# A hybrid encoder block on one core: three split weights in store, and a fourth Strassen pair in each FFN's second output part

## The chip, the cores and the metric

The kernel runs on one core of one Trainium2 chip. The metric is the device time of one execution in microseconds (us); the time of a kernel is the median of its runs.

## The reference, cut to what matters

One layer of an encoder with 256 tokens of width 2048, all in float32:

```python
h = layer_norm(ALPHA * h + 0.5 * swiglu_ffn(h, ffn1_w_in[l], ffn1_w_out[l]), ...)
mix = hybrid_mixer(h, w_in[l], ...)          # attention A, attention B, gates
h = layer_norm(ALPHA * h + mix, ...)
xa = memory_cross_attention(h, mem, ...)
h = layer_norm(ALPHA * h + xa, ...)
h = layer_norm(ALPHA * h + 0.5 * swiglu_ffn(h, ffn2_w_in[l], ffn2_w_out[l]), ...)

def swiglu_ffn(x, w_in, w_out):              # w_in 2048 x 11008, w_out 5504 x 2048
    g, u = jnp.split(x @ w_in, 2, axis=-1)
    return (jax.nn.silu(g) * u) @ w_out
```

## The kernel before, in words

Every weight is read once. A weight step is a tile `raw` of 128 x 2048 float32 (1 MB), loaded on SyncE's queue (L191, three buffers). ScalarE rounds it to `hi` in fp32r, two casts of 1024 columns (L262), and VectorE forms `lo = raw - hi` (L265). TensorE then computes hi x hi, hi x lo and lo x hi. The hi and lo of one step are a unit; `UNITS` (L51) is how many are held. Method `run` (L177) takes the list of steps in order and decides before each step which later weights are split already: at most `UNITS` units live, and at most two weights ahead of the next one. With two units that is one weight ahead of the one in use. A list scheduler then sets each engine's order from this program and the priorities.

An ordinary step (`mm_pair`, L301, matmuls at L309) handles two k-tiles for two column groups and both token halves: 24 matmuls of 512 columns. At some steps a Strassen form in Winograd's variant (`mm_sums`, L345, matmuls at L363) takes 21. For it VectorE forms sums of the weight's four blocks (`weight_sums`, L246 and L248), splits the weight's last 1536 columns and the 2048 of sums (`X` in the blocks X2 and X3), and forms sums of the activations (`sum_forms`, L319, L323, and L254 for their lo). Four of the seven products go to banks of their own; after the last Strassen step of a group they are copied and added (`shared`, L674 to L679), and then added to the residual (L628). The other matmuls gather in four banks, added to it at the end (`finish`, L749).

Each FFN (`ffn`, L551) has two halves of 24 and 19 k-tiles of its hidden width. A half is made of input groups (8 steps each, Strassen at 2, 4 and 6), whose products become hidden activations (`hidden`, L720 to L723), and of output parts. The second half's output is in two parts: the first 1024 columns by `out_pair` (L616) in ten steps of two k-tiles, the last of one, Strassen at 3, 5 and 7 (`SUMS_OUT`, L30); the other 1024 by `out_proj` (L755, matmuls at L296). The first part is what this document calls the output part; its activations' forms lie in the blocks X1 (steps 3 and 5) and X0 (step 7). `pair_group` (L643) walks the steps of a group in the order of the k-tiles.

Small tiles `w1` (128 x 256, L137) hold the totals of queries and keys, the rotary key's steps and some activations' forms. GpSimd issues the loads of biases, gains, rotary tables and memory tokens.

Of the kernel before, what the change touches and what calls it, by code (L numbers as in the profile page):

```python
# [27 lines left out]
SUMS_IN = {2: ("X0", 0), 4: ("X0", 1), 6: None}  # L28
AT_FIRST = 4, 6
SUMS_OUT = ({3: ("X1", 0), 5: ("X1", 1), 7: ("X0", 0), 9: ("X0", 1)},  # L30
            {3: ("X1", 0), 5: ("X1", 1), 7: ("X0", 0)})
SUMS_YB = {4: ("T0", 0), 6: ("T0", 1), 2: None}
AT_YB = (2, 4, 6), (4, 6)
SUMS_XQ = {4: ("H5", 0), 6: ("H5", 1), 2: None}
# [5 lines left out]
SUM_HOME = ("X2", "X3"),  # L40
# [7 lines left out]
RMS_EPS = 1e-6  # L48
NEG = -1e30
MAGIC = 0x5F3759DF  # L50
UNITS = 2  # L51
SOON, NEAR, LATE = 400, 100, -400
WARM = 9
HEADS = ("H4", "H5", "X2", "X3")
# [45 lines left out]
class Kernel:  # L100
    def __init__(self, ctx, tc, t, out):
        self.tc, self.nc, self.t, self.out = tc, tc.nc, t, out

        def pool(name, bufs=1, **kw):
            return ctx.enter_context(tc.tile_pool(name=name, bufs=bufs, **kw))

        self.const = pool("const")
        self.wraw = pool("wraw", 3)
        self.whi = pool("whi", UNITS)
        self.wlo = pool("wlo", UNITS)  # L110
        self.blocks = pool("blocks")
# [22 lines left out]
        return self.work.tile(list(shape), dt, tag="w2", bufs=6, name=self.name("w2"))  # L134

    def w1(self, shape=(P, S), dt=F32):
        return self.work.tile(list(shape), dt, tag="w1", bufs=6, name=self.name("w1"))  # L137

    def sm(self, tag, n, dt=F32, bufs=None):
        return self.small.tile([P, n], dt, tag=tag, name=self.name(tag), **({"bufs": bufs} if bufs else {}))  # L140
# [36 lines left out]
    def run(self):  # L177
# [3 lines left out]
        def slots(w):  # L181
            return 0 if isinstance(w, tuple) and w[1] else 1
# [35 lines left out]
        def early(w):  # L218
            return not isinstance(w, Sums) and w[1] is not None and "early" in w[1]

        def ahead(need, held):
            if nxt < need:
                return True
            n = sum(not early(w) for w in queue[need:nxt])
            return (nxt < need + 5 and (early(queue[nxt]) or n < 2)
                    and held + live + slots(queue[nxt]) <= UNITS)

# [323 lines left out]
    def ffn(self, tag, xT, st, first=None, steps=None, late=None, before=None, tags=None):  # L551


        t = self.t
        f0 = bank = 0
        turn = None
        fx = {}
        for half, nf in enumerate(F_SPLIT):
            hid, fh, homes = Act([]), {}, SUMS_OUT[half]
            end = half == len(F_SPLIT) - 1  # L560
            form = lambda c, fh=fh, homes=homes, hid=hid: self.forms_step(fh, homes, c, lambda: hid)
            for g in range(-(-nf // 4)):
                j, n = f0 // 4 + g, min(4, nf - 4 * g)
                qs, ps = {}, {}
                if j == 2 and first is not None:
                    self.add(self.load_rest)
                if j == 0 and first is not None:
                    main, (ps, qs, fx) = [], first
                    self.add(lambda qs=qs: self.shared(qs, 512), prio=SOON)
                elif j == 0 and before:  # L570
                    main = self.collect(self.first_group, tag, xT, before, ps, fx)
                else:
                    src = t[tag + "_w_in"][j] if n == 4 else t[tag + "_w_in_r"][0]
                    main = self.collect(self.pair_group, bank, src, n * P, KT, xT, SUMS_IN, fx, ps, qs, None, SUM_HOME + ("H5",))
                if turn and n < 4:
                    turn[5] = turn.pop(6)
                self.weave(main, turn or {}, prio=0)
                for c, (home, _) in homes.items():
                    if home == "X1" and c // 2 == g - 1:
                        self.add(form(c))  # L580
                hidden, turn = self.hidden(ps, bank, g, n, hid, qs)
                self.add(hidden, prio=SOON)
                if before and 2 <= j < 6:
                    self.add(lambda q=j - 2: self.gb_apply(2, self.h, (q,)), prio=LATE)
                if j == 0 and first is not None:
                    for c in set(SUMS_IN) - set(AT_FIRST):
                        self.add(self.forms_step(fx, SUMS_IN, c, xT, False))
                bank ^= 1
            if end and late:
                self.add(lambda: setattr(self, "cut", True))  # L590

            def out(hid=hid):
                x = lambda: hid
                src = [t[tag + "_w_out"][g, :, f0 * 1024:(f0 + nf) * 1024] for g in range(2)]
                self.out_pair(bank, src[0], 0, nf, x, homes, fh, half == 0, st if end else None,
                              SUM_HOME + ("H5",) if end else SUM_HOME)
                if end:
                    self.out_proj(tag + "_w_out_r", nf, x, False, st, steps, tags, 2, cut=tags is None)
                else:
                    self.out_pair(bank ^ 1, src[1], 1, nf, x, homes, fh, half == 0, None)  # L600
            main = self.collect(out)

            side = dict(turn)
            if end and late:
                side[len(main) - 6] = [late]
            for c, (home, k) in homes.items():
                if home == "X0":
                    side[4 + 2 * k] = side.get(4 + 2 * k, []) + [form(c)]
            if not end:
                for i in range(2):  # L610
                    side[len(main) - 3 + i] = [self.forms_step(fx, SUMS_IN, tuple(SUMS_IN)[i], xT)]
            self.weave(main, side, prio=0)
            turn = None
            f0 += nf

    def out_pair(self, bank, src, g, nk, x, at, fx, scale, st, sums_in=SUM_HOME):  # L616

        nc, h = self.nc, self.h
        ps, qs = {}, {}

        def shared():
            for (tt, a), s in qs["add"].items():
                c = (2 * g + a) * 512
                hs = h[tt][:, c:c + 512]
                if scale:
                    nc.vector.scalar_tensor_tensor(hs, hs, ALPHA, s, ALU.mult, ALU.add)
                else:
                    nc.vector.tensor_tensor(hs, hs, s, ALU.add)  # L628

        def finish():  # L630
            for tt in range(2):
                for a in range(2):
                    self.finish(tt, 2 * g + a, ps[tt, a], scale and not at, st)
        self.pair_group(bank, src, 512, nk, x, at, fx, ps, qs, shared, sums_in)
        self.add(finish)

    def group_tile(self, j):
# [2 lines left out]
    def group_tiles(self, j):  # L640
        return {(tt, g): self.group_tile(j) for tt in range(2) for g in range(2)}

    def pair_group(self, bank, src, n, nk, x, at, fx, ps, qs, then=None, sums_in=SUM_HOME):  # L643


        steps = -(-nk // 2)
        sums = [c for c in range(steps) if c in at]
        for c in range(steps):
            kts = range(2 * c, min(2 * c + 2, nk))
            ap = src[:, kts[0] * 2 * n:(kts[-1] + 1) * 2 * n]  # L650
            if c in at:
                def fn(w, c=c):
                    if c == sums[0]:
                        qs.update((a, self.group_tile(bank + 1)) for a in range(4))
                    self.mm_sums(ps, qs, w, n, x(), fx[c], 2 * c, c == sums[0], c == sums[-1])
                self.add(fn, Sums(ap, *sums_in))
                if c == sums[-1]:
                    self.add(lambda: self.shared(qs, n), prio=SOON)
                    if then:
                        self.add(then)  # L660
                continue

            def fn(w, c=c, kts=kts):
                if c == 0:
                    ps.update(self.group_tiles(bank))
                self.mm_pair(ps, w, n, x(), kts, c == 0, c == steps - 1)
            self.add(fn, ap)

    def shared(self, qs, n):
# [1101 lines left out]
```

## Time and profile before

| what | value |
|---|---|
| median of 3 runs | 2436.41 us (2433.37 to 2439.05) |
| span of the profiled execution | 2432.9 us |
| what lies around the span (median less span) | 3.5 us |
| TensorE busy, matmuls | 2423.0 us, 11286 |
| TensorE weight loads busy | 2022.5 us |
| VectorE busy | 2121.1 us |
| ScalarE busy | 1551.3 us |
| DMA | 516.20 MB, mean 212 GB/s |

The profile gives no total of its own for the profiled execution beside its span; the 3.5 us are the difference to the median of the runs. A row of a timeline has the start, the length, the engine, the line, and what it writes and reads, and then in brackets how long the engine was idle before it and what it waited for. A row of waits has who waited for whom, the sum in us, how many times and the longest.

### The profile page before, as it was taken

How to read it: one execution, taken by the hardware profiler on the slowest of the kernel's cores; microseconds unless marked ns; L12 is line 12 of the kernel's file. 1: busy time of each engine (PE TensorE's matmuls, PEld its weight loads, DVE VectorE, ACT ScalarE, POOL GpSimd, SP SyncE). 2: the span in 40 equal slices, each digit the busy share in tenths (PEclk: the TensorE clock that was granted, in tenths of full speed). 3: DMA queues.
4: the chain of work that ended last, by engine and by line, in shares of the span. 5: the costliest groups of instructions: out<-in, count | busy, mean ns of one | idle time of the engine just before them, and what ended most of it. 6: DMA issues, size and time to landing. Idle time of an engine off the chain costs nothing.

```text
span 2432.9 us, 29701 instructions
## 1 busy us (share of the span) xinstructions
PE 2423.0 (100%) x11286; PEld 2022.5 (83%) x11286; DVE 2121.1 (87%) x2423; ACT 1551.3 (64%) x2017; POOL 36.1 (1%) x81
## 2 busy tenths in 40 slices
PE   9999999999999999999999999999999999999999
PEld 8888888889888888888888888888888888888887
DVE  8999989899878898789788889979879999888997
ACT  6676745666555557878565687765666675556762
POOL 0000000000000001000000000000000000000000
PEclk9999999999999999999999999999999999999999
DMA  7766656666645657776577577655556666666665
GB/s 268 252 214 213 208 199 221 212 199 222 225 172 209 208 209 248 230 209 175 184 249 251 167 236 218 219 184 189 190 199 214 229 221 210 216 208 205 201 223 182
DMA packets 176414, 516.20 MB, mean 212 GB/s; under 512 B 111728, under 2 KB 112496, under 8 KB 121104
## 3 DMA queue, kind: packets, MB, share of 16 engines
q1 hardware_dynamic: 170816, 495.83, 61.2%
q0 software_dynamic: 4592, 17.30, 2.2%
q8 instruction: 88, 1.44, 0.2%
q10 hardware_dynamic: 864, 1.18, 0.1%
q14 instruction: 54, 0.44, 0.1%
HBM read 485.30 MB, written 2.10 MB: 200 GB/s over the span
## 4 chain that ended last, share of the span: by engine, by line
PE 90%; DVE 4%; ACT 3%; DMA 1%; issue 1%; SPq 0%; DVEq 0%; ACTq 0%
PE at L309 24%; PE mm L309 23%; PE mm L296 11%; PE at L363 10%; PE mm L363 10%; PE mm L275 5%; PE mm L277 2%; DVE lo L265 2%; ACT hi L262 1%; PE at L1028 1%; DMA raw<-w_xq 0%; PE at L1499 0%; PE at L1082 0%; PE at L275 0%; DMA raw<-w_o_b 0%
## 5 line engine op out<-in xcount | busy, mean ns | idle before, releaser
L262 ACT CAST hi<-raw 128x1024 fp32r<-128x1024 f32 (+1 forms) x852 | 805.3, 982 | 454.2 <-PE at L309 155.0
L265 DVE TENSOR_TENSOR lo<-raw,hi 128x2048 fp32r<-128x2048 f32 (+1 forms) x427 | 902.3, 2114 | 139.3 <-ACT hi L262 133.4
L309 PE MATMUL mm<-hi,T 128*128 128x512 f32 (+1 forms) x1328 | 311.1, 384 | 1.3 <-DVE v L397 1.3
L309 PEld LDWEIGHTS mm<-hi,T 128*128 128x128 f32 x1328 | 247.3, 188 | 48.5 <-DVE v L397 1.8
L309 PE MATMUL at<-hi,T 128*128 128x512 f32 x1152 | 275.5, 389 | 0.0
L262 ACT CAST X<-H 128x1024 fp32r<-128x1024 f32 (+1 forms) x166 | 170.6, 1034 | 162.0 <-DVE H L246 128.1
L309 PEld LDWEIGHTS at<-hi,T 128*128 128x128 f32 x1152 | 216.2, 188 | 45.1
L265 DVE TENSOR_TENSOR X<-H,X 128x2048 fp32r<-128x2048 f32 (+1 forms) x83 | 186.7, 2250 | 68.6 <-ACT X L262 68.6
L309 PE MATMUL mm<-lo,T 128*128 128x512 f32 (+1 forms) x664 | 160.4, 382 | 0.0
L309 PEld LDWEIGHTS mm<-lo,T 128*128 128x128 f32 x664 | 123.7, 188 | 22.8
L309 PE MATMUL at<-lo,T 128*128 128x512 f32 x576 | 142.4, 389 | 0.0
L309 PE MATMUL at<-hi,H 128*128 128x512 f32 x560 | 133.7, 389 | 0.0
L309 PEld LDWEIGHTS at<-lo,T 128*128 128x128 f32 x576 | 108.1, 188 | 22.5
L309 PEld LDWEIGHTS at<-hi,H 128*128 128x128 f32 x560 | 104.9, 188 | 21.6
L309 PE MATMUL mm<-hi,H 128*128 128x512 f32 x480 | 115.5, 391 | 0.3 <-DVE w L679 0.3
L248 DVE TENSOR_TENSOR H<-H,raw 128x512 f32<-128x512 f32 (+1 forms) x166 | 112.2, 676 | 2.2
L309 PEld LDWEIGHTS mm<-hi,H 128*128 128x128 f32 x480 | 89.5, 188 | 19.3 <-DVE w L679 0.8
L246 DVE TENSOR_TENSOR H<-raw 128x1024 f32<-128x1024 f32 (+1 forms) x83 | 99.4, 1198 | 0.9 <-DMA raw<-w_gate 0.8
L363 PE MATMUL mm<-X,X 128*128 128x512 f32 x342 | 91.1, 392 | 0.0
L262 ACT CAST X<-raw 128x1024 fp32r<-128x1024 f32 (+1 forms) x54 | 55.4, 1036 | 48.7 <-DVE raw L248 38.7
L363 PE MATMUL at<-X,X 128*128 128x512 f32 (+1 forms) x315 | 82.5, 386 | 0.9 <-DVE X L265 0.5
L849 ACT COPY w<-w 128x1024 uint16<-128x1024 uint16 (+1 forms) x60 | 75.8, 1276 | 0.6 <-DMA w<-w 0.5
(373 smaller groups left out, 4123.1 us busy)
## 6 DMA issues: line engine op xcount, KB each, us to landing
raw<-ffn_w_in SPq DMA_DIRECT2D x150, 1024.0 KB, 4.8
raw<-ffn_w_out SPq DMA_DIRECT2D x66, 1024.0 KB, 4.8
raw<-w_gate SPq DMA_DIRECT2D x32, 1024.0 KB, 4.8
raw<-ffn_w_out_r SPq DMA_DIRECT2D x16, 1024.0 KB, 4.9
raw<-w_qk SPq DMA_DIRECT2D x16, 1024.0 KB, 5.5
raw<-w_o_b SPq DMA_DIRECT2D x16, 1024.0 KB, 4.8
raw<-w_out SPq DMA_DIRECT2D x16, 1024.0 KB, 5.2
raw<-w_xk SPq DMA_DIRECT2D x16, 1024.0 KB, 5.3
```

Source lines behind the costliest of these rows:

```text
L246: self.nc.vector.tensor_tensor(two[0], two[1], raw[:, :m].unsqueeze(1).to_broadcast([P, 2, m]), ALU.add)
L248: self.nc.vector.tensor_tensor(t[:, a * m:a * m + m], t[:, b * m:b * m + m], raw[:, a * m:a * m + m], ALU.add)
L262: self.last_hi = self.nc.scalar.copy(hi[:, c:d], src[:, c:d])
L265: self.last_lo = self.nc.vector.tensor_tensor(lo[:, :n], src, hi[:, :n].bitcast(F32), ALU.subtract)
L275: self.nc.tensor.matmul(ps, hi[j], x.both(kt), start=(j == 0), stop=False)
L277: self.last_mm = self.nc.tensor.matmul(ps[:, :S], lo[j], x.at(0, kt), start=False, stop=(j == n - 1))
L296: self.last_mm = self.nc.tensor.matmul(ps, x.at(xi, kt)[:, tt * P:(tt + 1) * P], w[wi][:, j * 512 + c:j * 512 + c + m], start=(start and j ...
L309: self.last_mm = self.nc.tensor.matmul(ps[tt, g][:, :n], x.at(xi, kt)[:, tt * P:(tt + 1) * P], w[wi][:, c:c + n], start=first and j + wi + ...
L363: self.last_mm = self.nc.tensor.matmul(bank[:, :m], a[xi], v[wi][:, c * m:(c + 1) * m], start=own and first and wi + xi == 0, stop=own and ...
L849: self.nc.scalar.copy(self.words(u, n).rearrange("p (c k) -> p k c", k=2), self.words(s, n).rearrange("p (k c) -> p k c", k=2))
L1028: nc.tensor.matmul(ps[:, c0:c0 + nk], q[:, tt * P:(tt + 1) * P], k[:, :nk], start=(j == 0), stop=(j == len(parts) - 1))
```

## The change

It has three parts. [...] In the output part, step 1 becomes a fourth Strassen pair, and the steps run in the order 0, 2, 3, 4, 5, 6, 7, 8, 1, 9, so that step 1's forms can take the second half of X0. `pair_group` takes that order, starts its banks at the first and stops them at the last of it. The weights' layout in memory follows `SUMS_OUT`.

```diff
 SUMS_OUT = ({3: ("X1", 0), 5: ("X1", 1), 7: ("X0", 0), 9: ("X0", 1)},
-            {3: ("X1", 0), 5: ("X1", 1), 7: ("X0", 0)})
+            {3: ("X1", 0), 5: ("X1", 1), 7: ("X0", 0), 1: ("X0", 1)})
+ORDER_END = (0, 2, 3, 4, 5, 6, 7, 8, 1, 9)
-UNITS = 2
+UNITS = 3
     def w1(self, shape=(P, S), dt=F32):
-        return self.work.tile(list(shape), dt, tag="w1", bufs=6, name=self.name("w1"))
+        return self.work.tile(list(shape), dt, tag="w1", bufs=4, name=self.name("w1"))
                 self.out_pair(bank, src[0], 0, nf, x, homes, fh, half == 0, st if end else None,
-                              SUM_HOME + ("H5",) if end else SUM_HOME)
+                              SUM_HOME + ("H5",) if end else SUM_HOME, ORDER_END if end else None)
-    def pair_group(self, bank, src, n, nk, x, at, fx, ps, qs, then=None, sums_in=SUM_HOME):
-        steps = -(-nk // 2)
-        sums = [c for c in range(steps) if c in at]
-        for c in range(steps):
+    def pair_group(self, bank, src, n, nk, x, at, fx, ps, qs, then=None, sums_in=SUM_HOME, order=None):
+        order = range(-(-nk // 2)) if order is None else order
+        sums = [c for c in order if c in at]
+        for i, c in enumerate(order):
...
-            def fn(w, c=c, kts=kts):
-                if c == 0:
+            def fn(w, i=i, kts=kts):
+                if i == 0:
                     ps.update(self.group_tiles(bank))
-                self.mm_pair(ps, w, n, x(), kts, c == 0, c == steps - 1)
+                self.mm_pair(ps, w, n, x(), kts, i == 0, i == len(order) - 1)
-    nc = bacc.Bacc("TRN2", target_bir_lowering=False, num_devices=1)
+    nc = bacc.Bacc("TRN2", target_bir_lowering=False, num_devices=1, dynamic_dma_scratch_size=2048)
```

Lines of the changed kernel are one higher than before (L265 is L266). Numbers behind names tell buffers apart and differ between the two programs.

On VectorE, in FFN 1's output part, before: lo_4484 is step 2's, H_677 and lo_4519 are sums and lo of step 3 (the first Strassen pair), w_696 and w_697 the forms of step 7's activations, and X_681 is the lo of step 3's sums.

```order
L265 TENSOR_TENSOR lo_4484<-raw_4481,hi_4483 128x2048
L246 TENSOR_TENSOR H_677_4490<-raw_4488 128x1024
L265 TENSOR_TENSOR lo_4519<-raw_4488,hi_4518 128x1536
L248 TENSOR_TENSOR H_677_4490<-H_677_4490,raw_4488 128x512
L319 TENSOR_TENSOR w_696_4603<-H_655_4336 128x512
L323 TENSOR_TENSOR w_697_4604<-w_696_4603 128x128 x2
...
L265 TENSOR_TENSOR X_681_4524<-H_677_4490,X_680_4523 128x2048
L265 TENSOR_TENSOR lo_4557<-raw_4554,hi_4556 128x2048
```

And now, from step 2's lo_4415 to step 3's X_674; lo_4500 and lo_4537 are of steps 4 and 5:

```order
L266 TENSOR_TENSOR lo_4415<-raw_4412,hi_4414 128x2048
L247 TENSOR_TENSOR H_670_4421<-raw_4419 128x1024
L266 TENSOR_TENSOR lo_4460<-raw_4419,hi_4459 128x1536
L249 TENSOR_TENSOR H_670_4421<-H_670_4421,raw_4419 128x512
L266 TENSOR_TENSOR lo_4500<-raw_4497,hi_4499 128x2048
L249 TENSOR_TENSOR H_670_4421<-H_670_4421,raw_4419 128x512
L320 TENSOR_TENSOR w_698_4609<-H_655_4336 128x512
L266 TENSOR_TENSOR lo_4537<-raw_4504,hi_4536 128x1536
L266 TENSOR_TENSOR X_674_4465<-H_670_4421,X_673_4464 128x2048
```

Two lo of later steps have moved ahead of the lo of step 3's sums; most of the forms of step 7 have moved behind it.

On TensorE, in the same Strassen step, before: X_680 is the hi of the sums, X_681 their lo, hi_4556 step 4's weight.

```order
L363 MATMUL mm_4569<-X_680_4523,X_574_3824 128x512 x2
L363 MATMUL at_4455<-X_680_4523,H_561_3742 128x512 x2
L363 MATMUL mm_4568<-X_681_4524,X_574_3824 128x512
L363 MATMUL mm_4570<-X_681_4524,X_574_3824 128x512
L363 MATMUL mm_4569<-X_681_4524,X_574_3824 128x512
L363 MATMUL at_4455<-X_681_4524,H_561_3742 128x512
L309 MATMUL at_4453<-hi_4556,H_610_4055 128x512 x2
```

And now, with X_673 and X_674 for the sums and hi_4499 for step 4:

```order
L364 MATMUL mm_4548<-X_673_4464,X_574_3824 128x512 x2
L364 MATMUL at_4471<-X_673_4464,H_561_3742 128x512 x2
L310 MATMUL at_4469<-hi_4499,H_610_4055 128x512 x2
L310 MATMUL at_4470<-hi_4499,H_610_4055 128x512 x2
L310 MATMUL at_4472<-hi_4499,H_610_4055 128x512 x2
L310 MATMUL at_4469<-hi_4499,H_610_4055 128x512 x2
L364 MATMUL mm_4547<-X_674_4465,X_574_3824 128x512
L364 MATMUL mm_4549<-X_674_4465,X_574_3824 128x512
L364 MATMUL mm_4548<-X_674_4465,X_574_3824 128x512
L364 MATMUL at_4471<-X_674_4465,H_561_3742 128x512
```

Eight matmuls of step 4 have moved between the products with the sums' hi and those with their lo.

On SyncE's queue, at the first heads of attention B, before: `w_nope` are weights of heads, the transposes turn the heads' attention probabilities.

```order
L191 DMA raw_8393<-w_v 128x2048
L191 DMA raw_8400<-w_nope 128x2048
L191 DMA raw_8402<-w_nope 128x2048
L845 DMA_TRANSPOSE w_1292_8409<-H_1304_8464 128x6x128
L191 DMA raw_8519<-w_nope 128x2048
L845 DMA_TRANSPOSE w_1306_8476<-H_1304_8464 128x6x128
```

And now:

```order
L192 DMA raw_8444<-w_nope 128x2048
L192 DMA raw_8451<-w_nope 128x2048
L192 DMA raw_8453<-w_nope 128x2048
L846 DMA_TRANSPOSE w_1295_8420<-H_1312_8486 128x6x128
L846 DMA_TRANSPOSE w_1314_8498<-H_1312_8486 128x6x128
```

One more weight's load stands ahead of the first head's transpose, and the second transpose follows the first at once.

More of the change, by code (lines that the diff above doesn't have):

```diff
@@ L614, in ffn, with out_pair @@
             f0 += nf
-    def out_pair(self, bank, src, g, nk, x, at, fx, scale, st, sums_in=SUM_HOME):
+    def out_pair(self, bank, src, g, nk, x, at, fx, scale, st, sums_in=SUM_HOME, order=None):
         nc, h = self.nc, self.h
@@ L633, in finish @@
                     self.finish(tt, 2 * g + a, ps[tt, a], scale and not at, st)
-        self.pair_group(bank, src, 512, nk, x, at, fx, ps, qs, shared, sums_in)
+        self.pair_group(bank, src, 512, nk, x, at, fx, ps, qs, shared, sums_in, order)
         self.add(finish)
```

## The prediction

> **What bounds the kernel now.** I read the granted clock first, then the page's busy line, then TensorE's own waits, since a span that one engine fills can shrink only by less work on that engine or by less waiting in front of it.
>
> ```profile
> core 0: 2432.9 us, clock 1.000
> ```
>
> ```profile
> PE 2423.0 (100%) x11286; PEld 2022.5 (83%) x11286; DVE 2121.1 (87%) x2423; ACT 1551.3 (64%) x2017; POOL 36.1 (1%) x81
> ```
>
> The clock is whole, so no throttle hides in the numbers. PE is busy 2423.0 of 2432.9 us. The waits of PE, all of them, are these:
>
> ```profile
> PE mm L309 <- DVE v L397: 1.3, 1, 1.3
> PE at L490 <- DVE w L467: 1.1, 1, 1.1
> PE at L418 <- issue: 0.7, 1, 0.7
> PE at L363 <- DVE X L265: 0.5, 1, 0.5
> PE at L363 <- ACT X L262: 0.4, 2, 0.2
> PE mm L363 <- DVE T L254: 0.4, 1, 0.4
> PE mm L309 <- DVE w L679: 0.3, 1, 0.3
> PE at L1082 <- ACT H L849: 0.2, 1, 0.2
> PE mm L275 <- ACT hi L262: 0.2, 1, 0.2
> ```
>
> They add up to 5.1 us. Of these only 0.5 + 0.4 + 0.2 = 1.1 us wait for a weight's halves (lo and X from L265, hi from L262); 1.1 are the first matmul at the start and 0.7 a transpose behind the layer norm, which no weight store touches. So PE's count of matmuls is the bound, and everything that a third weight in store can return lies under 5.1 us.
>
> A step of TensorE can be read off the timeline: a Strassen step of FFN 1's second output part, and the ordinary pair and the output part that follow the last of them.
>
> ```profile
> 596.68 0.62 PE L363 MATMUL at<-hi,H 128*128 128x512 f32 x2
> ...
> 600.53 0.84 PE L363 MATMUL mm<-X,X 128*128 128x512 f32 x3
> ...
> 601.44 0.39 PE L309 MATMUL at<-hi,H 128*128 128x512 f32 x1
> ...
> 621.84 3.79 PE L309 MATMUL at<-hi,H 128*128 128x512 f32 x16
> 625.47 1.98 PE L309 MATMUL at<-lo,H 128*128 128x512 f32 x8
> 627.28 1.98 PE L309 MATMUL at<-hi,H 128*128 128x512 f32 x8
> ```
>
> The ordinary pair takes 627.28 - 621.84 = 5.44 us for its 24 matmuls, 0.227 each; the Strassen step 601.44 - 596.68 = 4.76 for 21, the same 0.227.
>
> VectorE is the second engine, and it is nearly full just there. The stretch of this output part, and the next one:
>
> ```profile
> 580.00:630.00 50.00, 50.00 (x223) 41.42 (x221) 46.41 (x49) 30.91 (x37) 0.00 (x0) 1.00 0.65 225
> 640.00:660.00 20.00, 20.00 (x90) 16.57 (x89) 11.09 (x6) 10.89 (x12) 0.00 (x0) 1.00 0.72 249
> ```
>
> Columns are PE, PEld, DVE, ACT, POOL. DVE has 3.6 us idle of 50 in the first, 8.9 of 20 in the second.
>
> **The matmuls.** One pair in each FFN goes from 24 to 21 matmuls: 2 x 3 x 0.227 = 1.36 us off an engine that never rests. The order lists six matmuls fewer, 20 instructions more on VectorE and six more on ScalarE, so the change does what it says. This term stands as long as nothing new waits.
>
> **VectorE's added work.** From the groups by form:
>
> ```profile
> L265 DVE TENSOR_TENSOR lo<-raw,hi 128x2048 fp32r<-128x2048 f32 x296 | 676.4, 2287 | 125.2 <-ACT hi L262 123.4 <-PE at L363 1.1
> L265 DVE TENSOR_TENSOR lo<-raw,hi 128x1536 fp32r<-128x1536 f32 x123 | 215.4, 1751 | 14.0 <-ACT hi L262 10.0 <-PE mm L309 3.3 <-PE at L309 0.4
> L265 DVE TENSOR_TENSOR X<-H,X 128x2048 fp32r<-128x2048 f32 x77 | 176.2, 2288 | 65.7 <-ACT X L262 65.7
> L248 DVE TENSOR_TENSOR H<-H,raw 128x512 f32<-128x512 f32 x154 | 105.6, 686 | 2.2
> L246 DVE TENSOR_TENSOR H<-raw 128x1024 f32<-128x1024 f32 x77 | 93.7, 1217 | 0.9 <-DMA raw<-w_gate 0.8
> L323 DVE TENSOR_TENSOR w<-w,w 128x128 f32<-128x128 f32 x78 | 22.0, 282 | 0.3
> L254 DVE TENSOR_TENSOR X<-w,X 128x512 fp32r<-128x512 f32 x26 | 17.6, 683 | 0.7 <-ACT X L253 0.5
> L319 DVE TENSOR_TENSOR w<-H 128x512 f32<-128x512 f32 x19 | 13.0, 682 | 0.0
> L262 ACT CAST X<-H 128x1024 fp32r<-128x1024 f32 x160 | 167.1, 1049 | 161.9 <-DVE H L246 128.1 <-DVE H L248 29.1 <-ACT hi L262 2.9
> ```
>
> Per FFN the weight costs 1.22 + 2 x 0.69 (sums) + 1.75 + 2.29 (two lo) - 2.29 (the lo it had) = 4.3 us, and the activations' forms 0.68 + 4 x 0.28 + 0.68 = 2.5, together 6.8 us. ScalarE gets two casts of 1.05 and small ones, and has 19 of 50 us free. Against DVE's 6.8 stand its 3.6 idle us in the stretch and the 8.9 after it. What may slip there: the additions of the products to h and the statistics, which PE does not await (the second part takes the banks of the copied products). So the total fits, and the question is whether one late lo meets PE.
>
> **The order of steps.** Step 1 leaves its place, so the first Strassen pair (3) comes one step, 5.44 us, sooner, while DVE is still at the hidden product of the last input group; its weight's load goes with it. The order shown with the change has two later lo, of pairs 4 and 5 (lo_4500, lo_4537), ahead of X_674, the lo of pair 3's sums, and on PE eight matmuls of pair 4 between X's hi and X's lo, which buy X_674 another 8 x 0.227 = 1.81 us. Where PE begins this part, and VectorE's pace there, before:
>
> ```profile
> 580.32 2.92 PE L309 MATMUL at<-hi,H 128*128 128x512 f32 x12
> ```
>
> ```profile
> 578.34 2.28 DVE L265 TENSOR_TENSOR lo<-raw,hi 128x2048 fp32r<-128x2048 f32 x1
> 580.54 0.55 DVE L676 TENSOR_TENSOR w<-w,at 128x384 f32<-128x384 f32 x1
> ...
> 583.06 0.55 DVE L721 TENSOR_TENSOR w<-w,mm 128x384 f32<-128x384 f32 x1
> 583.53 1.01 DVE L720 TENSOR_TENSOR w<-w,mm 128x384 f32<-128x384 f32 x2
> ...
> 586.66 1.02 DVE L723 SCALAR_TENSOR_TENSOR w<-w,w 128x384 f32<-128x384 f32 x2
> ```
>
> Starts follow each other 0.08 us sooner than durations say (578.34 to 580.54 is 2.20 for 2.28), so I add up pitches. X_674 is needed at 580.3 + 2 x 5.44 + (17 + 8) x 0.227 = 596.9. If DVE has nothing left but what had to wait for PE's last matmuls of the input group, it does four sums (1.9), two products (0.9), and the nine rows up to X_674 (2.20 + 1.14 + 1.67 + 0.60 + 2.20 + 0.60 + 0.60 + 1.67 + 2.20 = 12.9): 580.3 + 15.7 = 596.0, with half a microsecond for the activation in between 596.5. That is 0.4 us in time. If DVE is as late as before (L676 only at 580.54, 2.0 us of shared sums still ahead, and half of the stretch's 3.6 idle us on the way), X_674 ends at 580.5 + 2.0 + 15.7 + 1.7 = 599.9, 3.0 us late. With three units in store DVE can lie up to one step ahead as it enters, so I take the first end, with 0.1 us per FFN. For the later Strassen steps DVE has about 10.4 us of work per 10.2 of PE (a lo, a weight's 6.2, a form's 2), and 11.3 in the last stretch, with the turn of the hidden tiles and step 9's lo: no gain of ground, 0.2 + 0.2 + 1.1 us lost once it is behind.
>
> **The end of the part.** The last Strassen product now has only pair 9 (12 matmuls, 2.72 us) behind it, where it had 8.2 us. The second part's first bank is free with the copy of the first product, its second bank with that of the second, which it needs 4 matmuls, pair 9 and 12 more, 6.3 us, after that product is complete. Two casts of 1.05 us and a copy that is no longer than one of them stand before it on ACT. Cost nothing; without that cover, up to 2 us.
>
> **Three units.** The 1.1 us of weight waits should go; bound 0 to 1.1. Its other side is SyncE: a load is now issued a step earlier and stands ahead of transposes behind it. So it is in attention B's heads, as the order shows. The first head's transpose waits for one load more, and a load waits for a raw buffer, of which there are still three. Its user, L1082, waited 0.2 us before and comes about three heads later; 0 to 2 us, and I take 0.2.
>
> **Small tiles and the DMA scratch.** Four w1 tiles instead of six: the tightest place is the rotary key, whose first tile is read last by L1004 and is taken again, with four, by the second query-key total.
>
> ```profile
> 953.73 0.85 DVE L1004 TENSOR_TENSOR krope<-w,w 64x256 f32<-64x256 f32 x2
> 955.58 0.37 ACT L283 COPY w<-mm 128x256 f32<-128x256 f32 x1
> ```
>
> ```profile
> q0 software_dynamic: 4592, 17.30, 2.2%
> ```
>
> It is free at 954.58, 1.0 us ahead of the copy: nothing, bound 1 us. GpSimd's queue carries 4592 packets, 287 per DMA engine in the whole run, and its order does not change, so the smaller scratch gets 0, bound 1 us.
>
> Sum against the profiled span: 2432.9 - 1.36 - 1.1 + 0.2 + 0.2 = 2430.8. The median of the runs, 2436.41, is 3.5 over the span, taken as what lies around it: **2434.3 us**. Own range 2432.5 to 2436.
>
> **The rivals.** *VectorE becomes the bound in the output part.* It enters late, X_674 costs 3.0 us, and the later steps 0.2 + 0.2 + 1.1: 4.5 per FFN, 9.0 in all, less 1.36: 2444.0. For it: 46.4 of 50 busy and 6.8 to come. Against: the store of one more unit and PE's eight matmuls in between. It decides from DVE entering 0.9 us late, and makes the kernel slower by over 0.2% (4.9 us, about what a measurement can tell) from 3.1 us per FFN. Chance 0.11.
>
> *The gain is eaten.* Waits of 0.5 to 1.5 us at two or three places (out part, heads, a w1 tile) cancel 1.36: 2436.4. Chance 0.13.
>
> *All waits go.* The 3.3 us that are neither start nor layer norm end with the deeper store: 2436.4 - 1.36 - 3.3 = 2431.7, and less if the waits too short for that list go as well. Against: the 1.3 us sits behind statistics (L397), no weight. Chance 0.12.
>
> *PE has hidden bubbles.* PEld is busy 83%; if that were the measure of a full TensorE, 2432.9 - 2022.5 = 410 us would be open, and a store deeper by half might return tens: 2400 or less. But in 580 to 630, with PE's matmuls 0.227 apart and no wait, PEld is 41.42 of 50, 83% too: that is what full looks like. Chance 0.02. [...]
>
> **How the numbers follow.** Forecast 0.62, the rivals 0.11, 0.13, 0.12 and 0.02. Faster by over 0.2% needs under 2431.5: most of the third rival and the fourth, 0.12. Slower needs over 2441.3: the first, 0.11. Within 0.2%: 0.77. The range, 2430.5 to 2440.5, takes in forecast, eaten gain, most of the third rival and the milder half of the first.
>
> **What would show it.** In the changed profile PE should have six matmuls fewer, and the pair of step 1 should take 4.76 us; waits on L266 and L263 should be under 0.5 us; at the first Strassen step of each output part, PE should not wait for X. A wait of PE on DVE X there, or L1083 behind ACT, would prove me wrong; so would a span under 2427.

## The result, and the profile after

The changed kernel takes 2473.29 us (median of 4 runs, 2470.48 to 2475.20), the kernel before 2436.32 beside it: a ratio of 1.0155, interval 1.0141 to 1.0170. The change makes the kernel 37 us slower; the prediction was 2434.3 with a range to 2440.5. One execution of a later run took 6312.55 us where the others of the same kernel took under 2450; it is left out of the median given there.

The clock and the busy line of the changed kernel's page:

```profile
core 0: 2468.7 us, clock 0.998
```

```profile
PE 2429.3 (98%) x11280; PEld 2023.8 (82%) x11280; DVE 2131.9 (86%) x2443; ACT 1549.9 (63%) x2023; POOL 35.8 (1%) x81
```

The six matmuls are gone (11280 for 11286), yet PE is busy 6.3 us longer, at a clock that is no longer whole. VectorE has 10.8 us more (13.6 were forecast), ScalarE none. What has changed is PE's list of waits. These are its nine largest rows. Columns: who waited for whom, us in total, how often, the longest:

```profile
PE mm L276 <- DVE w L285: 8.0, 3, 7.3
PE mm L310 <- DVE w L680: 5.8, 7, 2.0
PE at L364 <- ACT X L263: 5.2, 5, 1.9
PE mm L310 <- DVE w L285: 2.7, 1, 2.7
PE mm L364 <- ACT X L263: 1.7, 2, 1.3
PE mm L364 <- DVE H L255: 1.7, 1, 1.7
PE at L310 <- DVE w L680: 1.5, 2, 0.9
PE mm L1538 <- DVE X L255: 1.2, 1, 1.2
PE mm L297 <- ACT T L254: 1.1, 2, 1.0
```

All 16 rows of that list add up to 34.7 us, where the list before had 5.1. So 34.7 - 5.1 = 29.6 us of waits and 2429.3 - 2423.0 = 6.3 us more of busy PE, whose matmuls are slower, make 35.9; the spans differ by 35.8.

The names tell what is waited for. L285 adds the two halves of a product out of a bank of PSUM (method `total`), and L680 is the last of the four sums by which `shared` frees the banks of a Strassen group: 18.0 us of the rows shown are PE waiting for a bank (8.0 + 5.8 + 2.7 + 1.5). Another 6.9 wait for the cast of a weight's sums (X from L263), and 4.0 of the rows shown, 5.6 of all 16, for the split of activations (L254, L255). No row of the list waits for hi of a weight. PE's own work comes late nowhere; what ScalarE and VectorE do behind a product, or beside it, does.

The longest wait, 7.31 us, in attention B. The timeline of the changed kernel, rows of PE, ScalarE and VectorE. The product `mm<-T,lo` is a head's query, and by the numbered names the sum at 1063.27 (L285) is the one that empties its bank, the oldest of the four in use, which the matmuls at 1063.74 take:

```profile
1047.16 2.07 PE L278 MATMUL mm<-T,lo 128*128 128x256 f32 x16
...
1057.02 1.98 ACT L263 CAST hi<-raw 128x1024 fp32r<-128x1024 f32 x2
1058.90 0.36 ACT L284 COPY w<-mm 128x256 f32<-128x256 f32 x1
1059.03 2.29 DVE L266 TENSOR_TENSOR lo<-raw,hi 128x2048 fp32r<-128x2048 f32 x1 [1.50 <-ACT hi L263]
...
1061.24 1.02 DVE L1056 SCALAR_TENSOR_TENSOR w<-at,X 128x384 f32<-128x384 f32 x2
...
1063.27 0.41 DVE L285 TENSOR_TENSOR w<-w,mm 128x256 f32<-128x256 f32 x1
...
1063.74 2.08 PE L276 MATMUL mm<-X,hi 128*128 128x512 f32 x4 [7.31 <-DVE w L285]
```

And the same product, copy and sum in the kernel before:

```profile
1038.47 2.07 PE L277 MATMUL mm<-T,lo 128*128 128x256 f32 x16
...
1041.49 0.36 ACT L283 COPY w<-mm 128x256 f32<-128x256 f32 x1
...
1044.95 0.41 DVE L284 TENSOR_TENSOR w<-w,mm 128x256 f32<-128x256 f32 x1
```

Before, the product ends at 1040.54, its copy begins 0.95 us later and its sum 4.4. Now it ends at 1049.23, the copy begins 9.7 us later, directly behind two casts of a later weight, and the sum 14.0 us later, behind the lo of that weight (2.29 us) and a softmax's scores. PE goes on with the three other banks until 1056.42, and then it must wait. Work for a weight that PE doesn't need yet stands ahead of the copy that it does need. The lo shows VectorE's order as well: VectorE is idle 1.50 us ahead of it, for its cast, while what the scores behind it read is there, the product since 1050.42 + 0.93 = 1051.35 (L1029) and the bias since 1053.02 + 0.34 = 1053.36 (L1045).

In the output part the four pairs do run as forecast. FFN 1, rows of PE: the products with the first Strassen pair's sums, step 1, and what follows it:

```profile
600.28 1.07 PE L364 MATMUL mm<-X,X 128*128 128x512 f32 x4
602.68 0.73 PE L364 MATMUL mm<-X,X 128*128 128x512 f32 x2 [1.34 <-ACT X L263]
...
631.00 0.61 PE L364 MATMUL at<-hi,H 128*128 128x512 f32 x2
...
635.76 1.98 PE L310 MATMUL at<-hi,H 128*128 128x512 f32 x8
637.57 1.07 PE L310 MATMUL at<-lo,H 128*128 128x512 f32 x4
638.48 1.75 PE L297 MATMUL mm<-hi,H 128*128 128x512 f32 x7
```

Step 1 takes 635.76 - 631.00 = 4.76 us for its 21 matmuls, and the second part begins at 638.48, just 0.91 after pair 9's last four matmuls started: the end of the part costs nothing. But the first pair waits 1.34 us for the hi of its sums (0.39 in FFN 2). What came before that hi, on VectorE and ScalarE:

```profile
599.34 0.69 DVE L249 TENSOR_TENSOR H<-H,raw 128x512 f32<-128x512 f32 x1
600.12 1.57 ACT L263 CAST hi<-raw 128x1024 fp32r<-128x1024 f32 x2 [4.08 <-DMA raw<-ffn_w_out]
601.59 1.04 ACT L263 CAST X<-H 128x1024 fp32r<-128x1024 f32 x1
```

The sums are complete at 600.03, while ScalarE stands idle. Next in its queue, though, are two casts of a later weight, for whose load it has waited 4.08 us, and the cast that PE needs comes behind them. This part is not where the 37 us are, but the same pattern stands behind the second cause below.

### The profile page after: what moved, and what is told of

Same layout as the page of the kernel before. It is cut to its first block, busy times and chain, and to the rows that moved or that the text cites. A ratio compares the mean times of both kernels' runs of the same rounds, so it can differ in the third digit from the quotient of the medians.

```text
span 2468.7 us, 29659 instructions
## 1 busy us (share of the span) xinstructions
PE 2429.3 (98%) x11280; PEld 2023.8 (82%) x11280; DVE 2131.9 (86%) x2443; ACT 1549.9 (63%) x2023; POOL 35.8 (1%) x81
## 4 chain that ended last, share of the span: by engine, by line
PE 71%; DVE 10%; ACT 8%; DMA 6%; issue 4%; SPq 0%; DVEq 0%; ACTq 0%
PE at L310 19%; PE mm L310 19%; PE mm L364 9%; PE at L364 9%; PE mm L297 8%; DVE lo L266 4%; ACT hi L263 4%; PE mm L276 3%; DMA raw<-w_xv 2%; PE mm L278 1%; DMA raw<-ffn_w_in 1%; ACT w L850 1%; PE at L1029 1%; ACT X L263 1%; DVE H L247 1%
## 5 line engine op out<-in xcount | busy, mean ns | idle before, releaser
L263 ACT CAST hi<-raw 128x1024 fp32r<-128x1024 f32 (+1 forms) x852 | 802.7, 981 | 539.3 <-PE at L310 102.5
L266 DVE TENSOR_TENSOR lo<-raw,hi 128x2048 fp32r<-128x2048 f32 (+1 forms) x427 | 902.8, 2115 | 170.9 <-ACT hi L263 160.6
L266 DVE TENSOR_TENSOR X<-H,X 128x2048 fp32r<-128x2048 f32 (+1 forms) x85 | 191.5, 2253 | 36.4 <-ACT X L263 36.3
L263 ACT CAST X<-H 128x1024 fp32r<-128x1024 f32 (+1 forms) x170 | 174.0, 1034 | 73.9 <-DVE H L249 47.4
L310 PE MATMUL at<-hi,H 128*128 128x512 f32 x528 | 126.9, 390 | 0.0
L310 PEld LDWEIGHTS at<-hi,H 128*128 128x128 f32 x528 | 98.8, 188 | 21.0 <-DVE w L680 0.4
L364 PE MATMUL mm<-X,X 128*128 128x512 f32 x360 | 96.1, 391 | 1.8 <-ACT X L263 1.7
L263 ACT CAST X<-raw 128x1024 fp32r<-128x1024 f32 (+1 forms) x54 | 55.0, 1035 | 59.2 <-DVE raw L249 29.5
L364 PEld LDWEIGHTS mm<-X,X 128*128 128x128 f32 x360 | 66.9, 188 | 17.9 <-ACT X L263 2.6
```

Source lines behind the costliest of these rows:

```text
L263: self.last_hi = self.nc.scalar.copy(hi[:, c:d], src[:, c:d])
L266: self.last_lo = self.nc.vector.tensor_tensor(lo[:, :n], src, hi[:, :n].bitcast(F32), ALU.subtract)
L310: self.last_mm = self.nc.tensor.matmul(ps[tt, g][:, :n], x.at(xi, kt)[:, tt * P:(tt + 1) * P], w[wi][:, c:c + n], start=first and j + wi + ...
L364: self.last_mm = self.nc.tensor.matmul(bank[:, :m], a[xi], v[wi][:, c * m:(c + 1) * m], start=own and first and wi + xi == 0, stop=own and ...
```

## The experiments

**First set: which of the change's parts is it?** Theory A: a weight split earlier than before puts its casts and its lo ahead of the copies and sums that free TensorE's banks, on two queues that ran in order where the traces show it (VectorE's 1.50 us above, ScalarE's 18.40 us below). Rival B: the fourth pair makes VectorE the bound. Rival C: four small tiles, or the small scratch, delay the copies.

*The third unit alone* (kernel before, no fourth pair):

```diff
-UNITS = 2
+UNITS = 3
-        return self.work.tile(list(shape), dt, tag="w1", bufs=6, name=self.name("w1"))
+        return self.work.tile(list(shape), dt, tag="w1", bufs=4, name=self.name("w1"))
-    nc = bacc.Bacc("TRN2", target_bir_lowering=False, num_devices=1)
+    nc = bacc.Bacc("TRN2", target_bir_lowering=False, num_devices=1, dynamic_dma_scratch_size=2048)
```

> The kernel before with the third unit alone (UNITS 3, four w1 tiles and the small scratch to make room; three Strassen pairs in the output part, old order of steps). Theory A, that a weight split two steps ahead puts its casts and its lo ahead of the copies and sums that free TensorE's banks on ScalarE's and VectorE's in-order queues: most of the loss is here, 2463 to 2475 us, with waits of PE on L284 and L679 as in the changed kernel. Rival B, that the fourth pair makes VectorE the bound: within 5 us of before, 2434 to 2441. Rival C, that four w1 tiles or the small scratch delay copies: as A here, so the next run tells them apart.

Measured: 2466.03 us, 1.0136 times before (1.0121 to 1.0151).

*The room alone*: the second and third of these edits, two units.

> The kernel before with only what made the room: four w1 tiles and the small scratch, two units. Theory A: 2434 to 2439 us, as before. Rival C (small tiles or scratch): 2446 or more, a third of the 37 us or more of it.

Measured: 2433.86 us, 0.9998 (0.9988 to 1.0007). C is out.

*The pair alone*: the changed kernel with `UNITS = 2`, six w1 tiles and the default scratch.

> The fourth pair and its order of steps alone, two units, six w1 tiles, the default scratch. Theory A: near before, 2433 to 2440 us: 1.4 us of matmuls gone, and as the store is no deeper some of the waits on X in the output part (6.6 us in the changed kernel) may stay. Rival B (VectorE bound through the fourth pair): 2450 or more.

Measured: 2435.07 us, 1.0004 (0.9995 to 1.0014). B is out. PE's matmuls there have the same six fewer, and the pair waits for its own weight in each FFN (0.7 us in two waits). The list scheduler has put two of its products with hi ahead of the last products of step 7. In FFN 1, on ScalarE and PE:

```profile
615.89 1.56 ACT L263 CAST hi<-raw 128x1024 fp32r<-128x1024 f32 x2
616.99 0.72 PE L364 MATMUL mm<-hi,H 128*128 128x512 f32 x2 [0.36 <-ACT hi L263]
```

*One weight ahead, three buffers*:

```diff
-                    and held + live + slots(queue[nxt]) <= UNITS)
+                    and held + live + slots(queue[nxt]) <= UNITS - 1)
```

> The changed kernel with all three buffers for hi and lo, but no weight split more than one step ahead (the limit on live units stays at two). Theory A: the loss is gone but for the pair's part, 2433 to 2440 us, and the third buffer does no harm by itself. Rivals B and C: still 2455 or more, as pair, tiles and scratch are all in.

Measured: 2464.60 us, 1.0131 (1.0114 to 1.0148). This is the number that B and C gave, but the three runs ahead of it put both out: the third unit alone carries the loss. And A's number is missed, since A had the wrong handle: how many weights ahead the program writes makes 6 of the 37 us at most; that there is a third *buffer* makes the rest. With the same program order as before, a cast may simply start sooner.

**Second set: which buffer, and is it the order?** With two buffers a cast must wait until PE has done with the unit two weights back. That wait was seen before on ScalarE's list (155.0 us behind L309 alone) and looked harmless, since ScalarE was busy only 1551.3 us, 64% of the span. Theory A sharpened: it was this wait that let the copies and sums go first.

*The third buffer for hi alone*, one weight ahead as in the run above:

```diff
-        self.wlo = pool("wlo", UNITS)
+        self.wlo = pool("wlo", UNITS - 1)
```

> As the run with three buffers and one weight ahead, but the third buffer for hi alone (lo has two). Theory A, now sharpened: it is the buffer, not the count of weights ahead, and of the two it is hi's: with two, ScalarE's cast had to wait for TensorE's last matmul with the unit before, and that wait let copies and sums go first; with three the cast is ready as soon as its weight has landed, and stands ahead of them. Then 2455 to 2470 us. Rival E, that it is lo's buffer (VectorE, the fuller engine, takes 2.3 us for each lo): 2433 to 2442.

Measured: 2448.50 us, 1.0059 (1.0044 to 1.0074), between the two ranges.

*The third buffer for lo alone* (`whi` has `UNITS - 1`):

> The same with the third buffer for lo alone (hi has two). Theory A (hi): 2433 to 2438 us, as with the fourth pair alone, since lo cannot start before its hi, which still waits. Rival E (lo): 2455 or more.

Measured: 2435.02 us, 1.0004 (0.9995 to 1.0014). So hi's third buffer costs 14.9 us, lo's alone nothing, and both together 30.8 (one weight ahead). Rival E is out, and A's number for hi alone was too high: lo's buffer adds 16 us once hi is free to run ahead.

*Casts and lo behind the last copy or sum*: three buffers, one ahead. `ev_a` and `ev_v` are the last ScalarE and VectorE instruction written in `total`, `shared` and `split`; `issue_after` places what follows it behind it on the same queue.

```diff
-            self.last_hi = self.nc.scalar.copy(hi[:, c:d], src[:, c:d])
+            with self.tc.issue_after(self.ev_a.ins) if self.ev_a is not None else nullcontext(): self.last_hi = self.nc.scalar.copy(hi[:, c:d], src[:, c:d])
...
+            with self.tc.issue_after(self.ev_v.ins) if self.ev_v is not None else nullcontext(): self.last_lo = self.nc.vector.tensor_tensor(lo[:, :n], src, hi[:, :n].bitcast(F32), ALU.subtract)
```

> Three buffers for hi and lo, one weight ahead, and each cast and each lo of a weight queued behind the last copy or sum that was written before it in the program (totals, shared products, splits of activations), on ScalarE and VectorE. Theory A (what overtakes is the cost): most of the loss returns, 2434 to 2446 us, with waits of PE on L284/L285 and L680 under 3 us together. Rival D (the third buffer costs by something other than the order in the queues: memory, DMA, transposes): still 2458 or more.

Measured: 2453.59 us, 1.0080 (1.0063 to 1.0097): 11 of 31 us return, less than A said and more than D allows. *The same two weights ahead*:

> The changed kernel, two weights ahead, with the same rule (casts and lo behind the last copy or sum written before them). Theory A: less returns than with one weight ahead, as a weight two steps ahead is written before the copies of two steps and so still overtakes the later one's: 2438 to 2460 us. Rival D: 2465 or more.

Measured: 2459.56 us, 1.0105 (1.0090 to 1.0120), inside A's range.

**Third set: what is left.** *The rule for totals and shared products only* (no `split`):

```diff
-        self.ev_a = copied = self.nc.scalar.copy(hi, src)
-        self.ev_v = self.nc.vector.tensor_tensor(lo, src, hi.bitcast(F32), ALU.subtract)
+        copied = self.nc.scalar.copy(hi, src)
+        self.nc.vector.tensor_tensor(lo, src, hi.bitcast(F32), ALU.subtract)
```

> As the run behind the last copy or sum, but the rule names only what frees TensorE's banks (totals and shared products), no longer the splits of activations. Theory A: the waits of PE on the weights' hi at the first Strassen steps of both FFNs (6.3 and 7.2 us in the stretches at 0 and 1900 us of that run, 3.1 and 0.1 before) were the splits' doing and go; the waits on totals and shared products stay gone: 2436 to 2450 us, and under 2453.6. Rival D (something other than the order): no better than 2453.

Measured: 2448.07 us, 1.0052 (1.0034 to 1.0070), against 1.0131 without the rule, and inside A's range. PE's waits on L285 and L680 fall from 20.6 us without the rule to 1.0. Waits on hi of weights, of which the run before had 4.1 us in all (fewer than the expectation says), are down to 0.2. The stretch with the longest wait, of the changed kernel and of this run (without the rule, with one weight ahead, that wait is 7.3 us as well); the second column is its length, then PE, PEld, DVE, ACT, POOL, the clock, and DMA:

```profile
1000.00:1100.00 100.00, 91.53 (x540) 76.47 (x539) 70.11 (x152) 70.65 (x144) 8.41 (x20) 0.97 0.68 208
```

```profile
1000.00:1100.00 100.00, 99.95 (x598) 84.23 (x597) 78.52 (x165) 75.41 (x157) 7.70 (x19) 1.00 0.81 230
```

And the head's query in this run, product, copy and sum:

```profile
1045.92 2.07 PE L278 MATMUL mm<-T,lo 128*128 128x256 f32 x16
...
1048.03 0.37 ACT L284 COPY w<-mm 128x256 f32<-128x256 f32 x1 [1.74 <-PE mm L278]
...
1048.53 0.41 DVE L285 TENSOR_TENSOR w<-w,mm 128x256 f32<-128x256 f32 x1
```

The product ends at 1047.99; the copy begins 0.04 us behind it and the sum 0.54. PE is full again. That is A shown for the banks: the same three buffers, the same work, another order, and 16.5 us less.

*Hi's third buffer alone, with this rule:*

> The third buffer for hi alone, with the rule of the run before (casts and lo behind totals and shared products). Theory A: below the 2448.5 us of the third hi buffer alone, 2434 to 2446. Rival D: 2446 to 2452, as without the rule, since what is left there (waits on casts of sums and on lo) is no wait on a bank.

Measured: 2451.93 us, 1.0081 (1.0061 to 1.0102). No gain over 2448.5, as D said: the 15 us of hi's buffer are not of this kind. A fails here, and a second cause is needed. *No weight ahead*, to put the casts behind the copies by the program's order (`UNITS - 2` in the limit):

> The changed kernel with three buffers for hi and lo and no weight ahead in the program: a step's casts and lo are written behind the whole step before, so the list puts them behind its copies where both are ready. Theory A: waits on totals, shared products and casts of sums shrink, waits on weights come in their place: 2434 to 2455 us, under the 2464.6 with one ahead. Rival D: 2462 or more.

Measured: 2521.15 us, 1.0357 (1.0341 to 1.0373), outside both. Its longest wait shows a second cause, in an extreme case. VectorE, ScalarE and PE; the H<-X cast is the second of a weight's sums:

```profile
1302.49 1.41 DVE L249 TENSOR_TENSOR X<-X,raw 128x512 f32<-128x512 f32 x2
...
1320.40 1.04 ACT L263 CAST hi<-raw 128x1024 fp32r<-128x1024 f32 x1 [18.40 <-DMA raw<-w_o_b]
1321.35 1.04 ACT L263 CAST H<-X 128x1024 fp32r<-128x1024 f32 x1
...
1322.44 1.22 PE L364 MATMUL mm<-H,T 128*128 128x512 f32 x2 [14.86 <-ACT H L263]
```

The sums are ready at 1303.90. Their second cast stands in ScalarE's queue behind a cast of another weight that is still being loaded; ScalarE stands idle for 18.40 us, and PE for 14.86, for a cast of one microsecond that lacked nothing. The wait is this long because that load came late: 18.40 us of waiting for it alone are 3.8 times the 4.9 us that the median load of its kind took in this run from issue to landing. Why it came late is not shown.

**Fourth set: does the load cost, and where?** ScalarE's waits of casts, of the kernel before, the changed one, hi's third buffer alone, and the run below:

```profile
ACT hi L262 <- PE at L309: 155.0, 77, 5.0
...
ACT hi L262 <- DMA raw<-ffn_w_in: 3.7, 3, 2.0
```

```profile
ACT hi L263 <- PE at L310: 102.5, 53, 3.7
ACT hi L263 <- DMA raw<-ffn_w_in: 92.9, 37, 4.9
```

```profile
ACT hi L263 <- DMA raw<-ffn_w_in: 133.3, 56, 4.9
ACT hi L263 <- PE at L310: 78.7, 37, 3.7
```

```profile
ACT hi L263 <- PE at L310: 103.4, 61, 3.9
...
ACT hi L263 <- DMA raw<-ffn_w_in: 16.1, 8, 2.8
```

Over all rows of this kind, casts waited for PE 361.7, 256.5, 214.5 and 285.5 us, and for loads 47.5, 206.1, 320.9 and 77.3. The wait for PE was the harmless one: it ends when PE has moved on. Once the buffer is free, the next limit is the load, and there are three buffers for loads.

*Hi's third buffer with a fourth raw buffer*, in the room of the third lo:

```diff
-        self.wraw = pool("wraw", 3)
+        self.wraw = pool("wraw", 4)
```

> The third buffer for hi alone and a fourth raw buffer in the room of the third lo. With the third hi buffer ScalarE's casts wait less on TensorE (362 us in the kernel before, 215 with hi's third buffer) and more on loads that have not landed (48 us before, 321). Theory F, that it is this wait on a load, with the sums' casts and the copies behind it in the queue, that costs: a load can start one weight sooner, the waits on loads fall under 150 us, and the loss of 14.9 us falls by half or more: 2434 to 2441 us. Theory A (what overtakes costs by its own length and place): casts that are ready still sooner overtake more, 2446 to 2460.

Measured: 2435.42 us, 1.0005 (0.9995 to 1.0014). The 15 us are gone, and the waits on loads are 77 us, as theory F said. A's range is missed. *The whole room for raw buffers*, two units, five raw:

> The fourth pair with two units, and the whole room of the third unit given to raw buffers (five). The cast still has to wait for TensorE's last matmul with the unit before last. Theory A: as the pair alone, 2432 to 2437 us; the room does no harm where it does not free the casts. Theory F: the same or 1 to 2 us less, 2431 to 2435. If it is 2445 or more, both are wrong, and any work that is ready sooner harms.

Measured: 2435.84 us, 1.0008 (0.9999 to 1.0018), inside A's range and just over F's. Casts waited 14.3 us for loads there, and 401.6 for PE: what holds them is PE again, and more raw buffers neither harm nor help.

*Casts in the order written*, added to the rule for totals and shared products (`issue_after(self.last_hi.ins)` around each cast):

> As the run behind totals and shared products, and the casts of weights besides in the order in which they are written, so that no cast of a later weight goes ahead of the cast of an earlier one's sums. Theory A: the waits on the sums' casts (4.7 us there) go for the most part, 2438 to 2446 us. Rival: a cast that waits for VectorE's sums now holds the casts behind it, which come late to TensorE: 2448 to 2475, with waits on hi.

Measured: 2444.57 us, the median of three runs (2444.51 to 2449.93), 1.0053 (1.0036 to 1.0069), inside A's range. The waits on the sums' casts are gone from PE's list (4.7 us before), and other waits, for lo and for a bank, have taken their place, 14.5 us in all against 16.1. The 3.5 us under 2448.07 are less than the runs of either kernel scatter, so a gain is not shown. On ScalarE the casts of hi now wait 83.9 us for loads instead of 214.1, but the casts of sums 228.4 us for VectorE instead of 104.5: the queue stops for something else.

*Half the rule each*. Only lo behind the last sum:

> Three buffers for hi and lo, one weight ahead, only each lo queued behind the last total or shared product on VectorE; casts are free. Theory G (two parts: 15 us come with hi's third buffer, through casts that stand in ScalarE's queue before their load has landed, and 16 more with lo's third, through work of later weights that overtakes what frees TensorE's banks). If the overtaking that costs is that of lo on VectorE: 2446 to 2452 us, as with both rules. If it is that of the casts on ScalarE: 2456 to 2466, as without a rule.

Measured: 2453.71 us, 1.0086 (1.0070 to 1.0103). Only casts behind the last copy:

> The other half: only the casts queued behind the last total's or shared product's copy on ScalarE; lo is free. If the overtaking on VectorE costs by itself: 2456 to 2466 us. If ScalarE's casts lead and a lo only follows its cast: 2444 to 2452, as with both rules.

Measured: 2453.23 us, 1.0080 (1.0065 to 1.0095). Both lie between the two ranges that were given. Each half returns 11 of the 31 us, both together 16.5. Neither queue is the one culprit.

**What follows.** Of the loss, the pair, the small tiles and the scratch make nothing that can be measured. The third hi buffer costs 15 us with three raw buffers and nothing with four: a cast is no longer held by PE but by its load, and holds ScalarE's queue. The third lo buffer on top costs another 16, returned by an order that puts the emptying of banks first. What stays open: a fourth raw buffer changes the list scheduler's order too, so that the 15 us are only shown to hang on the number of raw buffers; that they are spent in queues behind a waiting cast is shown at two places (the first pair of the output part, where PE waited 1.34 us, and the late load above, 14.86 us), and argued for the rest. Nor does the time follow the waits on loads alone: with the casts in the order written these are 83.9 us, near the 77.3 of the fourth raw buffer, and the kernel is still 11 us slower than before. Three buffers of hi and of lo with four of raw were not tried. Of the runs with the pair the nearest (2435.02, 1.0004) cannot be told from the kernel before, and none beats it.

## Why the prediction was wrong

**The bound, right.** PE's count of matmuls is the bound of the kernel before. From it I concluded that a deeper store can give little, which holds, but not that it can take little, which doesn't.

**The matmuls, right in size.** Six fewer, 4.76 us for step 1. Alone the change of steps gives 2435.07 against 2433.84; the 1.36 us are not seen, and 0.7 of them went to a wait for the pair's own hi.

**VectorE's added work and the order of steps, right in kind, 1.3 us short in FFN 1 and 0.4 in FFN 2.** I had X_674, the lo, for the critical one, with eight matmuls of cover; what came late was the second cast of X's hi, on ScalarE, 1.34 us, behind two casts of a later weight. This was a rival's place (VectorE the bound, 9.0 us), but not its engine, and far from its price.

**The end of the part, small tiles, scratch: right.** 638.48 follows without a gap; the room alone is 0.9998 (0.9988 to 1.0007). That the scratch bears on GpSimd's queue, and by how much the change makes it smaller, no run shows; what the runs show is this one ratio, for tiles and scratch together.

**Three units: the step that failed.** It said: the 1.1 us of weight waits go, bound 0 to 1.1, and "its other side is SyncE", 0.2 us taken out of 0 to 2. I looked for the other side on one queue only, and in one place, attention B's heads. It lay on ScalarE's and VectorE's queues, all over the kernel: 32 us by the run with the third unit alone, 31 by the one with one weight ahead, 37 in the changed kernel. (The unit's 32 and the pair's 1 make 33; what the other 4 are is not shown.) The wait behind the transposes for which it took the 0.2 us is not in the new list at all. The rows that told of the loss stood beside the diff. I showed two lo of later pairs moved ahead of the lo that PE needs, priced that for the output part alone, and then counted the deeper store in VectorE's favour ("DVE can lie up to one step ahead as it enters"). A weight that is split early is split ahead of something, and here that something waited: the copy of the head's query 9.7 us for 0.95, its sum 14.0 for 4.4. ScalarE's own list of waits, which I did not weigh, held the other half: 155.0 us of casts waiting for PE's L309 look like idle time of an engine off the bound, and so like nothing. They were the release of a buffer that kept the order.

**The weight waits, 1.1 us.** Of these the 0.2 on hi went, the 0.5 on X from L265 became 0.8, and the 0.4 on X from L262 became 6.9.

**The rivals.** The gain eaten at two or three places was the right mechanism (a wait that takes the place of another) with a size of 1.4 us instead of 30. That all waits go was the opposite of what happened: 5.1 us became 34.7. PE's hidden bubbles stay refuted: with PE 99.95 of 100 us busy, PEld is 84.23.

## What to carry to other kernels

A buffer pool's size can set more than how far ahead work runs: with two buffers here, the release by the consumer (361.7 us of waits of casts, 256.5 with three) was also what kept the work for later loads behind the consumer's own follow-up on ScalarE's and VectorE's queues. Before a pool is made deeper, list for every engine what the early work will now stand ahead of, price the worst of these for each stage and not only where the change is aimed, and ask which resource holds the early work next; if that is a transfer, look for a queue that stops for it, as ScalarE's did here for 18.40 us. Deepen the pools in front of it too, or pin the order of what empties the accumulators: here the first returned the 15 us of hi's buffer and the second 16.5 of 31, and neither beat the kernel before.

## What the runs showed of the hardware

Between the changed kernel's first and last matmul the clock fell in a long wait, and once just behind a short one. Windows of the changed kernel around the 7.31 us wait, around one of 1.66 us at 1461, and around two of 2.00 and 2.72 us; columns as in the windows above:

```profile
1056.00:1063.70 7.70, 0.43 (x4) 0.22 (x2) 6.20 (x12) 5.18 (x10) 0.00 (x0) 0.81 0.96 311
1063.70:1067.70 4.00, 3.96 (x12) 3.34 (x13) 2.65 (x11) 4.00 (x11) 0.00 (x0) 0.52 0.64 244
...
1461.00:1463.40 2.40, 0.50 (x2) 0.19 (x2) 2.40 (x3) 2.16 (x3) 0.00 (x0) 1.00 0.83 335
1463.40:1467.40 4.00, 4.00 (x11) 3.13 (x12) 4.00 (x4) 1.57 (x2) 0.00 (x0) 0.57 0.32 78
...
1530.00:1534.00 4.00, 4.00 (x18) 3.31 (x19) 4.00 (x6) 3.58 (x4) 0.00 (x0) 1.00 0.35 65
1625.50:1629.00 3.50, 0.78 (x4) 0.34 (x3) 3.50 (x5) 3.37 (x6) 0.00 (x0) 1.00 0.92 305
1629.00:1633.00 4.00, 4.00 (x19) 3.29 (x20) 2.93 (x3) 2.00 (x3) 0.00 (x0) 1.00 0.86 334
```

After the 7.31 us the next 4.0 us run at 0.52, after the wait at 1461 at 0.57, while 2.00 and 2.72 us leave the clock whole. Such a wait so costs a second time: 4.0 x 0.48 = 1.9 us for the longest, and 4.0 x 0.43 = 1.7 for the other. That is an estimate of 3.6 for the 6.3 us that PE is busy longer; the rest is not traced.

At 1461 PE was never idle for two microseconds at a stretch, and the clock fell as well. The trace shows more: the clock is at half (0.50) from 1060.74 for 6.83 us and from 1463.51 for 3.41 us, and these four changes lie 6.83, 395.95 and 3.41 us apart, which is 2, 116 and 1 times 3.413. In the 3.41 us ahead of the two falls PE was busy 0.00 and 1.27 us; in the stretches of the same grid with the waits of 2.00 and 2.72 us, from 1528.37 and 1627.35, it was busy 1.94 and 1.92 us, and the clock stayed. So here the longest gap does not tell where the clock fell (1.66 us before a fall, 2.72 before none), and the busy share of these four stretches does: 0.00 and 0.37 against 0.57 and 0.56. That the share is what sets the clock is not shown.
